# Attention of a two-layer trunk on one core: the products behind the maxima taken for two neighbouring heads at once, each in 64 rows of the contraction

## The chip, the core and the metric

The kernel runs on one core of a Trainium2 chip. Its time is the device time of the whole program in microseconds (us), median of three runs. The engines are named as the profile names them: PE is the matrix engine (PEld its weight loads), DVE the vector engine, ACT the scalar engine, POOL GpSimd, SP the sync engine. All numbers of the program are 32-bit floats. Where an operand has the type `F32R`, PE multiplies in one pass and in reduced precision, and the kernel makes up for that by splitting a value into a high and a low part. Where it has the type `F32`, one product is two passes, which the trace shows as two matmuls.

## What is computed

The reference is a trunk of two layers over 1024 latent tokens (and 256 context tokens) of width 1024. Layer 0 is an mLSTM and convolution mixer, layer 1 is attention, and each has an MLP behind it. The change lies in the attention, which is this:

```
def gqa_attend(q, k, v):
    bsz, nq, _, _ = q.shape
    qg = q.reshape(bsz, nq, KV_HEADS, ATT_HEADS // KV_HEADS, HEAD_DIM)
    s = jnp.einsum('bqhgd,bkhd->bhgqk', qg, k).astype(jnp.float32) * HEAD_DIM ** -0.5
    p = jax.nn.softmax(s, axis=-1).astype(v.dtype)
    o = jnp.einsum('bhgqk,bkhd->bqhgd', p, v)
    return o.reshape(bsz, nq, ATT_HEADS * HEAD_DIM)
```

There are 16 query heads of 64 numbers, 4 key heads (four query heads share one) and 1280 keys: the 1024 latent tokens and the 256 of the context.

## The kernel before

The queries are projected first, in the part of the program that is called the projection below (the loops `for g in range(4)` and `for keep in (2, 1, 0)`, lines 1509 to 1536). `queries` writes each head to `q_d` in device memory as 128 rows: 64 rows of high parts and 64 rows of low parts. The keys lie in `kst[c][:, kv, 0, :]`, where the same 64 high parts stand twice, in rows 0 to 63 and in rows 64 to 127. So one matmul over 128 rows gives (high + low of q) times (high of k).

The attention itself, called the stage below, goes over 32 blocks. A block is one head and one half of the queries: 512 queries against all 1280 keys. Softmax needs the maximum of each query's scores before the exponentials, and the kernel gets it from products of its own, the **score matmuls** of `score` (line 1392): for each group of 128 queries (four of them) and each piece of the keys (`TBS`: 512, 512 and 256 keys) one matmul into a PSUM tile `s`, and one DVE reduction `nm<-s` of that tile to the negated maximum. That is 12 score matmuls and 12 reductions per block: 8 of 512 keys and 4 of 256. `top_of` joins the three pieces, and `rows_of` turns the result into four rows of the operand `qb` (a small F32 matmul `s<-ident,top` into another `s` tile, and a DVE multiply `qb<-s,ident`). The products that the exponentials are taken from, `st`, then carry the subtraction of the maximum inside them.

A block is worked off in five steps (`n` counts all steps, `p` those of a block); a step handles two of the ten key tiles:

- `scores` issues some score matmuls of the next block, as far as the table `BY` allows. It is called at the step's start, once before the first half of `attend`, and once before the second half.
- `part` subtracts the high part of the exponentials of the step before from them, on DVE, where that step is one of `ON_DVE` (p = 1, 3); for the others `probs` gave the subtraction to POOL (`pt<-pf,pt`).
- `probs` issues four `st` matmuls, the exponential `pf<-st` and its rounded copy `pt<-pf` on ACT.
- `attend` issues six `av` matmuls, three per half, for the step three steps back (`LAG`). The second of each three has only 64 columns of weights (`vst[:, at_, 2, :]`).
- At a block's end, ACT takes `av` out of PSUM; after every second block `keep` finishes two heads (`of<-of` on DVE, among others).

So PE has four `st` and six `av` matmuls in every step, 50 in a block, each with 512 columns. They are called **wide matmuls** below.

`InOrder` (`pe_`, `dve_`, `act_`, `pool_`) keeps the instructions of the stage in the order in which the code issues them. The projection and the loads of queries (`load_q`, on POOL's queue) are placed by a scheduler. PSUM has eight banks of 512 numbers per row. In the stage two hold `s` tiles (pool `s`, two buffers of one bank), four hold `st`, two hold `av`. A tile's buffer is given out again when the last reader of its former content is done.

Of the kernel before, what the change touches and what calls it, by code (L numbers as in the profile page):

```python
# [46 lines left out]
def trunk(ctx, tc, a, out):  # L47
    nc = tc.nc
    sp, act, dve, pool, pe = nc.sync, nc.scalar, nc.vector, nc.gpsimd, nc.tensor

    def opened(name, bufs=1, space=None, side=None):
        kw = {"space": space} if space is not None else {}
        if side is not None:
            kw["side"] = side
        return tc.tile_pool(name=name, bufs=bufs, reuse_waits="tile", **kw)
# [4 lines left out]
    hl_pool = ctx.enter_context(opened("hl", 8))  # L60
# [33 lines left out]
    pe_, dve_, act_, pool_ = (InOrder(e) for e in (pe, dve, act, pool))  # L94
# [423 lines left out]
    for half in (1, 0):  # L518
        n = 264
# [307 lines left out]
    for n in range(-3, nv + 3 + BACK):  # L827
# [13 lines left out]
        if done:  # L841
            r = done.pop(0)
# [544 lines left out]
    ap_ = at.enter_context(opened("att", 1, side="right"))  # L1387
    kst = [ap_.tile([P, 4, 2, TBS[b][1]], F32R, name=f"kst{b}") for b in range(3)]
    vst = ap_.tile([P, NTT * 4, 3, 64], F32R, name="vst")
    q_d = dram.tile([16, P, SEQ], F32, name="q_d")  # L1390

    def score(k, qa_, nm, ps, pe, dve):

        i, qt, c = k // 12, k // 3 % 4, k % 3
        kv, n = i % 16 // 4, TBS[c][1]
        pe.matmul(ps[:, 0:n], qa_[:, qt * P:(qt + 1) * P], kst[c][:, kv, 0, :], start=True, stop=True)
        dve.tensor_reduce(out=nm[:, qt, c:c + 1], in_=ps[:, 0:n], axis=AX.X, op=ALU.max, negate=True)

    with opened("rope", 1, side="right") as rp:
        tab = hc_pool.tile([P, 2, 2, 8, 64], F32, name="tab", tag="hc")  # L1400
# [108 lines left out]
        for g in range(4):  # L1509
            wc = load_cols(w_in, 256 * g, 256, dve)  # L1510
            for tt in range(8):
                pq = psum()
                proj_tok(pq, wc, h, tt, 256)
                q2 = heads(pq, tt, 0)
                later(lambda q2=q2, g=g, tt=tt: queries(q2, g, tt), 3)
                if g * 8 + tt < NTT:
                    fill(g * 8 + tt)
                if (g, tt) == (3, 0):
                    ahead = raw_pool.tile([P, 2, 512], F32R, name="ahead", tag="raw")
                    nm0 = ap_.tile([P, 4, 3], F32, name="nm0")  # L1520
                    pool.dma_start(out=ahead, in_=q_d[0:2, :, 0:512].rearrange("h p t -> p h t"))
                if g == 3:
                    for k in range((12 - TAIL) * tt // 8, (12 - TAIL) * (tt + 1) // 8):
                        score(k, ahead[:, 0], nm0, psum(), pe, dve)
                    if tt == 8 - AFTER:
                        wv = load_cols(w_in, 1280, 256)
        k = 12 - TAIL
        for keep in (2, 1, 0):
            if AFTER > 2 - keep:
                pv = psum()  # L1530
                proj_tok(pv, wv, h, 7 - (2 - keep), 256)
                values(7 - (2 - keep), pv)
            later(keep=keep)
            for k in range(k, k + TAIL // 3):
                score(k, ahead[:, 0], nm0, psum(), pe, dve)
            k += TAIL // 3 > 0


# [2 lines left out]
    ps_ctx.close()  # L1541
    wctx.close()
    o_t = [[act_pool.tile([P, KT, 512], F32R, name=f"o{b}{s}", tag="act") for s in "hl"] for b in range(2)]
    with opened("s", 2, PSUM) as scp, opened("st", 2, PSUM) as stp, opened("av", 2, PSUM) as avp, \
            opened("prob", 4, side="right") as bp, opened("sm", 4, side="right") as sm:
        blocks = [(b, hd) for b in range(2) for hd in range(16)]
        nb = len(blocks)
        qa, qb, nms, avs, pts = {}, {}, {}, {}, {}

        def load_q(i):  # L1550
            b, hd = blocks[i]
            qa[i] = bp.tile([P, 512], F32R, name="qa", tag="qa", bufs=3)
            pool.dma_start(out=qa[i], in_=q_d[hd, :, b * 512:(b + 1) * 512])
            nms[i] = sm.tile([P, 4, 3], F32, name="nm", tag="nm")

        def copy_q(i):
            b, hd = blocks[i]
            qb[i] = bp.tile([68, 512], F32R, name="qb", tag="qb", bufs=3)
            act_.copy(out=qb[i][0:64], in_=qa[i][0:64])

        def top_of(i):
            nm = nms[i]
            nms[i] = sm.tile([P, 4], F32, name="top", tag="top")
            dve_.tensor_reduce(out=nms[i], in_=nm, axis=AX.X, op=ALU.min)

        def rows_of(i):

            tp = scp.tile([P, 512], F32, name="s", tag="s")
            pe_.matmul(tp[64:68, 0:P], nms.pop(i), ident, start=True, stop=True)
            dve_.tensor_tensor(out=qb[i][64:68].rearrange("p (j t) -> p j t", j=4), in0=tp[64:68, 0:P].unsqueeze(1).broadcast_to([4, 4, P]),  # L1570
                               in1=ident[64:68, 64:68].unsqueeze(2).broadcast_to([4, 4, P]), op=ALU.mult)

# [51 lines left out]

        NP, LAG, WAIT, ON_DVE = NTT // 2, 3, 1, (1, 3)

        BY = (5, 7, 10, 12, 14)
        outs, ofs, early = [], {}, []
        qa[0], qa[1], nms[0] = ahead[:, 0], ahead[:, 1], nm0
        nms[1] = sm.tile([P, 4, 3], F32, name="nm", tag="nm")  # L1630
        copy_q(0)
        top_of(0)
        rows_of(0)
        pairs = [(i, p) for i in range(nb) for p in range(NP)]
        k = 12

        def scores(upto, n):
            nonlocal k
            for _ in range(n):
                if k < min(upto, 12 * nb):  # L1640
                    score(k, qa[k // 12], nms[k // 12], scp.tile([P, 512], F32, name="s", tag="s"), pe_, dve_)
                    k += 1

        for n in range(len(pairs) + LAG):
            i, p = divmod(n, NP)
            upto = 12 * (i + 1) + BY[p]
            if p == 1 and i + 2 < nb:
                load_q(i + 2)
            if p == 2 and i + 1 < nb:
                copy_q(i + 1)  # L1650
            if (i, p) == (nb - 2, 0):
                early.extend(load_raw(kt_view(a["att_w_out"][0], m * P, P), [KT, P]) for m in range(2))
            if p == 4 and i + 1 < nb:
                top_of(i + 1)
            scores(upto, 1)
            if n and n <= len(pairs):
                part(*pairs[n - 1])
            if n < len(pairs):
                probs(i, p)
# [131 lines left out]
```

## Time and profile before

| what | value |
|---|---|
| time, median of 3 runs | 2942.59 us (2941.59 to 2946.01) |
| the profiled execution's own time | 2953.12 us |
| its span, first to last instruction | 2951.4 us |
| the stage, from 1714 to 2198 us of the span | 484 us |
| PE busy over the span | 96% |
| mean granted clock of PE | 0.974 of full speed |

The page lists each engine's busy time, and further views split it by stretch, by line and by tile. PE's matmuls overlap, so the duration of one (some 0.39 us for a wide one) is longer than the distance from its start to the next one's start. That distance is what a matmul costs PE, and it is read from the timeline. All instructions of the stage stand under line 92, the helper that `InOrder` is made of, so they are told apart by their tiles.

### The profile page before, as it was taken

The page shows a single profiled execution, that of the slowest core. Times are in us where ns is not written, and L with a number is a line of the kernel's source. Part 1 is how long each engine was busy: PE and PEld are TensorE (multiplying, and loading weights), DVE is VectorE, ACT ScalarE, POOL GpSimd, SP SyncE. Part 2 cuts the span into 40 slices and gives each one's busy share as a digit, 9 for nine tenths or more (in the row PEclk, how much of TensorE's full clock was granted, in tenths as well). Part 3 has the DMA queues.
Part 4 walks back from the last instruction along what each step waited for, and adds up shares of the span by engine and source line. Part 5 has one row for each costly group of instructions (what it writes and reads, how often), then busy time and mean ns, then how long its engine had stood idle before and what let it go on. Part 6 is the DMA issues. An engine that isn't in the chain of part 4 may idle for free. (4 is left out here: it accounts for less than half of the span.)

```text
span 2951.4 us, 39291 instructions
## 1 busy us (share of the span) xinstructions
PE 2827.4 (96%) x14523; PEld 2328.2 (79%) x14523; DVE 2030.5 (69%) x3376; ACT 1492.9 (51%) x2556; POOL 691.2 (23%) x564
## 2 busy tenths in 40 slices
PE   7999999988999999999999999999999899989999
PEld 4788998777788888888888977777778688878887
DVE  5445672779876668778787777777756865568886
ACT  5311223455444444444556568888875555544443
POOL 2222424511000000000035545655554000000000
PEclk8999999898999999999999999999999899999999
DMA  6121651344666676332241310000025354474423
GB/s 236 56 73 45 202 153 51 108 146 127 195 190 188 181 243 241 110 136 93 79 144 50 100 52 19 18 19 19 19 80 160 93 175 147 133 288 157 157 93 107
DMA packets 194834, 360.19 MB, mean 122 GB/s; under 512 B 15206, under 2 KB 83666, under 8 KB 194642
## 3 DMA queue, kind: packets, MB, share of 16 engines
q1 hardware_dynamic: 179970, 312.59, 31.4%
q0 software_dynamic: 14672, 45.10, 6.0%
q8 instruction: 114, 1.87, 0.3%
q14 instruction: 78, 0.64, 0.1%
HBM read 260.53 MB, written 97.10 MB: 121 GB/s over the span
## 5 line engine op out<-in xcount | busy, mean ns | idle before, releaser
L338 PE MATMUL ps<-w 128*128 128x512 f32 (+1 forms) x1152 | 424.9, 369 | 0.8 <-DVE w L102 0.8
L339 PE MATMUL ps<-w 128*128 128x512 f32 (+1 forms) x1152 | 424.4, 369 | 0.0
L337 PE MATMUL ps<-w 128*128 128x512 f32 (+1 forms) x1152 | 389.8, 370 | 9.3 <-ACT w L101 9.3
L337 PE MATMUL ps<-tb,w 128*128 128x512 f32 x883 | 351.9, 399 | 15.2 <-ACT u L957 6.2
L339 PE MATMUL ps<-tb,w 128*128 128x512 f32 x888 | 349.6, 397 | 4.0 <-DVE w L102 4.0
L338 PE MATMUL ps<-tb,w 128*128 128x512 f32 x888 | 352.6, 397 | 0.0
L348 DVE SCALAR_TENSOR_TENSOR xT<-ps,mod,xT 128x512 f32<-128x512 f32 (+1 forms) x392 | 255.3, 693 | 87.9 <-PE ps L339 87.5
L92 DVE TENSOR_REDUCE nm<-s 128x1 f32<-128x512 f32 x372 | 217.4, 599 | 106.7 <-PE s L92 101.2
L101 ACT CAST w<-ssum 128x512 fp32r<-128x512 f32 x256 | 155.4, 619 | 258.5 <-PE ps L339 230.7
L92 POOL TENSOR_TENSOR pt<-pf,pt 128x1024 fp32r<-128x1024 f32 x96 | 230.4, 2400 | 171.4 <-ACT pt L92 168.2
L92 PE MATMUL av<-pt,vst 128*128 128x512 f32 (+1 forms) x960 | 257.7, 394 | 0.8 <-POOL pt L92 0.8
L337 PEld LDWEIGHTS ps<-w 128*128 128x128 f32 x1152 | 217.3, 189 | 48.8 <-ACT w L101 10.7
L338 PEld LDWEIGHTS ps<-w 128*128 128x128 f32 x1152 | 218.0, 189 | 40.1 <-DVE w L102 1.2
L339 PEld LDWEIGHTS ps<-w 128*128 128x128 f32 x1152 | 217.3, 189 | 37.7
L906 POOL DMA_DIRECT2D raw<-in_mlp_w_dram x70 | 62.3, 890 | 646.0 <-DVE w L102 301.5
L337 PEld LDWEIGHTS ps<-tb,w 128*128 128x128 f32 x883 | 168.4, 191 | 52.7 <-ACT u L957 7.5
L339 PEld LDWEIGHTS ps<-tb,w 128*128 128x128 f32 x888 | 169.0, 190 | 44.4 <-DVE w L102 5.8
L92 PEld LDWEIGHTS av<-pt,vst 128*128 128x128 f32 (+1 forms) x960 | 159.4, 171 | 56.3 <-POOL pt L92 1.2
L92 ACT ACTIVATE pf<-st 128x1024 f32<-128x1024 f32 x160 | 164.2, 1026 | 75.5 <-PE st L92 68.5
L213 DVE SCALAR_TENSOR_TENSOR aacc<-araw,cw,aacc 128x512 f32<-128x512 f32 x196 | 149.4, 794 | 73.9 <-DMA araw<-in_ada_w_dram 73.3
L338 PEld LDWEIGHTS ps<-tb,w 128*128 128x128 f32 x888 | 169.6, 191 | 35.0
L102 DVE TENSOR_TENSOR w<-ssum,w 128x512 fp32r<-128x512 f32 x256 | 172.5, 682 | 16.3 <-ACT w L101 14.6
(388 smaller groups left out, 6651.8 us busy)
## 6 DMA issues: line engine op xcount, KB each, us to landing
hid<-c SPq DMA_DIRECT2D x224, 256.0 KB
tf<-hid SPq DMA_DIRECT2D x112, 512.0 KB
araw<-in_ada_w_dram SPq DMA_DIRECT2D x72, 512.0 KB
raw<-in_mlp_w_dram POOLq DMA_DIRECT2D x70, 512.0 KB, 5.0
park<-xT SPq DMA_DIRECT2D x32, 512.0 KB
xT<-park SPq DMA_DIRECT2D x32, 512.0 KB
w2e<-in_mlp_w_dram SPq DMA_DIRECT2D x32, 512.0 KB
w2o<-in_mlp_w_dram SPq DMA_DIRECT2D x32, 512.0 KB
```

The costliest lines, as they stand in the source:

```text
L92: return lambda *args, **kw: tc.keep_in_program_order(op(*args, **kw))
L101: (hi_eng or act.copy)(out=hi, in_=src)
L102: (lo_eng or pool).tensor_tensor(out=lo, in0=src, in1=hi.bitcast(F32), op=ALU.subtract)
L213: dve.scalar_tensor_tensor(out=accs[w], in0=r[:, k, :], scalar=c, in1=accs[w], op0=ALU.mult, op1=ALU.add)
L337: pe1.matmul(ps, whi, hhi, start=start, stop=False, skip_group_check=goes_on)
L338: pe.matmul(ps, whi, hlo, start=False, stop=False, skip_group_check=goes_on)
L339: pe.matmul(ps, wlo, hhi, start=False, stop=stop, skip_group_check=goes_on)
L348: dve.scalar_tensor_tensor(out=xT[b][:, m, :], in0=ps[:, 0:n], scalar=mod[layer][:, gate * 8 + m, w:w + 1], in1=xT[b][:, m, :], op0=ALU.mu ...
L906: pool.dma_start(out=r, in_=kt_view(w1, (2 * p + e) * P, P))
```

## The change

`score` now takes the maxima of two neighbouring heads. A tile `qm` of 128 rows holds the high parts of head 2j in rows 0 to 63 and those of head 2j + 1 in rows 64 to 127 (`load_qm`: two loads of 64 rows from `q_d`). Two matmuls, one on each half of the rows, take the place of two on all 128 rows; the low parts of q no longer go into the maximum. The two write the two banks of one `s` tile, and in the stage one DVE reduction reads both and gives both maxima. In the projection there are two `psum` tiles and two reductions.

What goes with it:

- Pool `s` has one buffer of two banks instead of two buffers of one. `rows_of` takes the same buffer.
- The scores run one pair of heads ahead: those of blocks 0 and 1 in the projection (12 pairs of matmuls, where 12 single ones were), and those of blocks 2j + 2 and 2j + 3 while blocks 2j and 2j + 1 are worked off. `BY` has ten entries, one per step of two blocks (`r`). The calls of `scores` are two per step: at its start, and between the halves of `attend`.
- `top_of` runs once for two blocks. `qa` and `qb` have two buffers instead of three, `load_q` is called for the next block instead of the one after it, and `qm` has two buffers. The projection's `qm0` takes a buffer of the pool `hl`.

```
-    def score(k, qa_, nm, ps, pe, dve):
-
-        i, qt, c = k // 12, k // 3 % 4, k % 3
+    def score(k, qm, nm, ps, pe, dve):
+
+
+        i, qt, c = k // 12 * 2, k // 3 % 4, k % 3
         kv, n = i % 16 // 4, TBS[c][1]
-        pe.matmul(ps[:, 0:n], qa_[:, qt * P:(qt + 1) * P], kst[c][:, kv, 0, :], start=True, stop=True)
-        dve.tensor_reduce(out=nm[:, qt, c:c + 1], in_=ps[:, 0:n], axis=AX.X, op=ALU.max, negate=True)
+        for e in range(2):
+            es = slice(e * 64, e * 64 + 64)
+            pe.matmul(ps[e][:, 0:n], qm[es, qt * P:(qt + 1) * P], kst[c][es, kv, 0, :], start=True, stop=True)
+        for e, p in enumerate(ps) if isinstance(ps, list) else ():
+            dve.tensor_reduce(out=nm[:, e, qt, c:c + 1], in_=p[:, 0:n], axis=AX.X, op=ALU.max, negate=True)
+        if not isinstance(ps, list):
+            dve.tensor_reduce(out=nm[:, :, qt, c], in_=ps[2][:, :, 0:n], axis=AX.X, op=ALU.max, negate=True)
+
+    def load_qm(j, qm):
+
+        b, hd = j // 8, j % 8 * 2
+        for e in range(2):
+            pool.dma_start(out=qm[e * 64:(e + 1) * 64], in_=q_d[hd + e, 0:64, b * 512:(b + 1) * 512])
...
-    with opened("s", 2, PSUM) as scp, opened("st", 2, PSUM) as stp, opened("av", 2, PSUM) as avp, \
+    with opened("s", 1, PSUM) as scp, opened("st", 2, PSUM) as stp, opened("av", 2, PSUM) as avp, \
...
-        BY = (5, 7, 10, 12, 14)
+        BY = (1, 3, 4, 5, 7, 8, 9, 11, 12, 12)
...
-                if k < min(upto, 12 * nb):
-                    score(k, qa[k // 12], nms[k // 12], scp.tile([P, 512], F32, name="s", tag="s"), pe_, dve_)
+                if k < min(upto, 6 * nb):
+                    s = scp.tile([P, 2, 512], F32, name="s", tag="s")
+                    score(k, qms[k // 12], nms[k // 12], (s[:, 0], s[:, 1], s), pe_, dve_)
                     k += 1
...
-            upto = 12 * (i + 1) + BY[p]
-            if p == 1 and i + 2 < nb:
-                load_q(i + 2)
+            j, r = divmod(n, 2 * NP)
+            upto = 12 * (j + 1) + BY[r]
+            if p == 1 and 2 <= i + 1 < nb:
+                load_q(i + 1)
+            if r == 6 and 2 * j + 4 < nb:
+                load_pair(j + 2)
...
-            scores(upto, 1)
             if n >= LAG:
                 attend(*pairs[n - LAG], 0)
-            scores(upto, 9)
+            scores(upto)
```

Within two blocks the twelve pairs are numbered 0 to 11 below; pairs 2, 5, 8 and 11 have 256 keys, the others 512. The new table puts this many wide matmuls of PE between one pair and the next: 10 from pair 0 to 1, 7 to pair 2, 3 to pair 3, 10 to pair 4, 10 to pair 5; then 4, the first `top` matmul, and 3 to pair 6; 3 to pair 7, 10 to pair 8, 10 to pair 9, 7 to pair 10, 3 to pair 11; then 14, the second `top` matmul, and 6 to the next pair 0.

PE at the end of a block's last `st` matmuls, before: one `top` matmul, then single score matmuls, and up to six wide ones between them.

```order
L92 MATMUL s<-ident,top 4x128 [waits DVE_49]
L92 MATMUL s<-kst_13927,qa 128x512 [waits DVE_49]
L92 MATMUL av<-pt,vst 128x512
L92 MATMUL av<-pt,vst 64x512
L92 MATMUL av<-pt,vst 128x512 x2
L92 MATMUL av<-pt,vst 64x512
L92 MATMUL av<-pt,vst 128x512
L92 MATMUL s<-kst_13928,qa 128x256 [waits DVE_49]
L92 MATMUL st<-qa,kst_13926 128x512 [waits Activation_49]
```

The same place now, at the middle of two blocks: the `top` matmul and pairs 6 and 7, each of which waits for DVE with its first matmul.

```order
L92 MATMUL s<-ident,top 4x128 [waits DVE_49]
L92 MATMUL av<-pt,vst 128x512
L92 MATMUL av<-pt,vst 64x512
L92 MATMUL av<-pt,vst 128x512
L92 MATMUL s<-kst_13926,qm 128x512 [waits DVE_49]
L92 MATMUL s<-kst_13926,qm 128x512
L92 MATMUL av<-pt,vst 128x512
L92 MATMUL av<-pt,vst 64x512
L92 MATMUL av<-pt,vst 128x512
L92 MATMUL s<-kst_13927,qm 128x512 [waits DVE_49]
L92 MATMUL s<-kst_13927,qm 128x512
```

What moved: the score matmuls now come in pairs with three wide matmuls between them here, and all of them, with the `top` matmul, pass through one buffer.

DVE over the same stretch, before: `pt` is `part`'s subtraction and `qb` the multiply of `rows_of`.

```order
L92 TENSOR_TENSOR pt<-pf,pt 128x1024 [waits Activation_49,Pool_49]
L92 TENSOR_TENSOR qb<-s,ident 4x512 [waits PE_49]
L92 TENSOR_REDUCE nm<-s 128x1 [waits PE_49] x7
L92 TENSOR_TENSOR pt<-pf,pt 128x1024 [waits Activation_49,Pool_49]
L92 TENSOR_REDUCE nm<-s 128x1 [waits PE_49] x4
```

And now, from pair 4's reduction to pair 11's:

```order
L92 TENSOR_REDUCE nm<-s 128x2 [waits PE_49]
L92 TENSOR_TENSOR of<-of 128x512 [waits Activation_49]
L92 TENSOR_REDUCE nm<-s 128x2 [waits PE_49]
L92 TENSOR_TENSOR pt<-pf,pt 128x1024 [waits Activation_49,Pool_49]
L92 TENSOR_TENSOR qb<-s,ident 4x512 [waits PE_49]
L92 TENSOR_REDUCE nm<-s 128x2 [waits PE_49] x4
L92 TENSOR_TENSOR pt<-pf,pt 128x1024 [waits Activation_49,Pool_49]
L92 TENSOR_REDUCE nm<-s 128x2 [waits PE_49] x2
```

What moved: half as many reductions, each of two maxima. `pt`, `qb` and `of` still stand between them, and the buffer that they hold up is the only one.

## Rows read from the trace of the kernel before

**Rows 1.** Busy time of each engine in a stretch: the projection's end, and 100 us of the stage.

```profile
core 0: us, PE busy (x) PEld busy (x) DVE busy (x) ACT busy (x) POOL busy (x), PEclk, DMA share, GB/s
1640.00:1714.00 74.00, 69.08 (x568) 68.28 (x566) 55.34 (x98) 35.79 (x102) 38.51 (x62) 0.98 0.32 92
1760.00:1860.00 100.00, 98.63 (x429) 72.26 (x429) 71.73 (x111) 83.49 (x94) 58.85 (x30) 1.00 0.07 19
```

**Rows 2.** Timeline of PE: the `top` matmul of two blocks, 22 blocks apart.

```profile
1774.23 0.38 PE L92 MATMUL s<-ident,top 128*4 128x128 f32 x2
...
2103.00 0.38 PE L92 MATMUL s<-ident,top 128*4 128x128 f32 x2
```

**Rows 3.** Timeline of PE, and matmuls by form: wide matmuls and a score matmul of 256 keys.

```profile
1801.37 0.28 PE L92 MATMUL s<-kst,qa 128*128 128x256 f32 x1
1801.49 1.55 PE L92 MATMUL av<-pt,vst 128*128 128x512 f32 x6
1802.88 0.40 PE L92 MATMUL s<-kst,qa 128*128 128x512 f32 x1
...
L92 PE MATMUL av<-pt,vst 128*64 128x512 f32 x320 | 126.2, 394 | 0.0
```

**Rows 4.** Timeline of PE around one `top` matmul.

```profile
1803.82 0.40 PE L92 MATMUL st<-qb,kst 68*128 68x512 f32 x1
1804.15 0.38 PE L92 MATMUL s<-ident,top 128*4 128x128 f32 x2
1804.46 0.50 PE L92 MATMUL s<-kst,qa 128*128 128x512 f32 x1
1804.79 0.40 PE L92 MATMUL av<-pt,vst 128*128 128x512 f32 x1
```

**Rows 5.** Timeline of PE early in the program: full matmuls, then 32-column ones.

```profile
109.82 0.40 PE L339 MATMUL ps<-h0h,wlo 128*128 128x512 f32 x1
110.15 0.62 PE L170 MATMUL ps<-raw,cw 128*32 128x512 f32 x2
...
147.62 0.28 PE L339 MATMUL ps<-h2h,wlo 128*128 128x256 f32 x1
147.83 0.62 PE L170 MATMUL ps<-raw,cw 128*32 128x512 f32 x2
```

**Rows 6.** Timeline of PE in layer 0: F32 matmuls on 64 rows and on 128.

```profile
520.87 0.27 PE L775 MATMUL ps<-cn,aq 64*128 64x129 f32 x1
521.07 0.49 PE L773 MATMUL ps<-va,ub 128*128 128x129 f32 x2
521.49 0.37 PE L775 MATMUL ps<-cn,aq 64*128 64x129 f32 x1
521.50 0.37 PE L733 MATMUL ps<-qT,kT 64*128 64x128 f32 x1
```

**Rows 7.** DVE's groups in the stage, 1714 to 2198 us.

```profile
L92 DVE TENSOR_REDUCE nm<-s 128x1 f32<-128x512 f32 x248 | 170.7, 689 | 97.1 <-PE s L92 95.4
L92 DVE TENSOR_TENSOR pt<-pf,pt 128x1024 fp32r<-128x1024 f32 x64 | 78.4, 1225 | 14.3 <-ACT pt L92 11.5 <-issue 0.3
L92 DVE TENSOR_TENSOR of<-of 128x512 f32<-128x512 f32 x15 | 16.9, 1124 | 21.1 <-ACT of L92 21.1
```

**Rows 8.** Timeline of DVE beside rows 3 and 4.

```profile
1801.69 0.42 DVE L92 TENSOR_REDUCE nm<-s 128x1 f32<-128x256 f32 x1 [0.37 <-PE s L92]
...
1803.32 0.69 DVE L92 TENSOR_REDUCE nm<-s 128x1 f32<-128x512 f32 x1 [1.00 <-PE s L92]
...
1805.41 0.69 DVE L92 TENSOR_TENSOR qb<-s,ident 4x512 fp32r<-4x512 f32 x1
```

**Rows 9.** Timeline of PE's weight loads: the first that waits for that `qb`.

```profile
1806.15 0.19 PEld L92 LDWEIGHTS s<-kst,qa 128*128 128x128 f32 x1 [0.23 <-DVE qb L92]
```

**Rows 10.** POOL's loads of queries: time on POOL, KB and us to landing.

```profile
L1553 POOL DMA_DIRECT2D qa<-q_d x27 | 15.3, 569 | 26.5 <-PE st L92 25.0 <-PE s L92 1.5
...
qa<-q_d POOLq DMA_DIRECT2D x30, 256.0 KB, 3.0
```

**Rows 11.** Timeline of PE where the stage begins.

```profile
1714.09 0.38 PE L92 MATMUL s<-ident,top 128*4 128x128 f32 x2 [2.40 <-DVE top L92]
```

More of the change, by code (lines that the diff above doesn't have):

```diff
@@ L1519, in trunk @@
                     ahead = raw_pool.tile([P, 2, 512], F32R, name="ahead", tag="raw")
-                    nm0 = ap_.tile([P, 4, 3], F32, name="nm0")
+                    nm0 = ap_.tile([P, 2, 4, 3], F32, name="nm0")
+                    qm0 = hl_pool.tile([P, 512], F32R, name="qm0", tag="hl")
+                    load_qm(0, qm0)
                     pool.dma_start(out=ahead, in_=q_d[0:2, :, 0:512].rearrange("h p t -> p h t"))
@@ L1523, in trunk @@
                     for k in range((12 - TAIL) * tt // 8, (12 - TAIL) * (tt + 1) // 8):
-                        score(k, ahead[:, 0], nm0, psum(), pe, dve)
+                        score(k, qm0, nm0, [psum(), psum()], pe, dve)
                     if tt == 8 - AFTER:
@@ L1534, in trunk @@
             for k in range(k, k + TAIL // 3):
-                score(k, ahead[:, 0], nm0, psum(), pe, dve)
+                score(k, qm0, nm0, [psum(), psum()], pe, dve)
             k += TAIL // 3 > 0
@@ L1547, in trunk, with load_pair, top_of @@
         nb = len(blocks)
-        qa, qb, nms, avs, pts = {}, {}, {}, {}, {}
+        qa, qb, qms, nms, tops, avs, pts = {}, {}, {}, {}, {}, {}, {}
         def load_q(i):
             b, hd = blocks[i]
-            qa[i] = bp.tile([P, 512], F32R, name="qa", tag="qa", bufs=3)
+            qa[i] = bp.tile([P, 512], F32R, name="qa", tag="qa", bufs=2)
             pool.dma_start(out=qa[i], in_=q_d[hd, :, b * 512:(b + 1) * 512])
-            nms[i] = sm.tile([P, 4, 3], F32, name="nm", tag="nm")
+        def load_pair(j):
+            qms[j] = bp.tile([P, 512], F32R, name="qm", tag="qm", bufs=2)
+            load_qm(j, qms[j])
+            nms[j] = sm.tile([P, 2, 4, 3], F32, name="nm", tag="nm")
         def copy_q(i):
             b, hd = blocks[i]
-            qb[i] = bp.tile([68, 512], F32R, name="qb", tag="qb", bufs=3)
+            qb[i] = bp.tile([68, 512], F32R, name="qb", tag="qb", bufs=2)
             act_.copy(out=qb[i][0:64], in_=qa[i][0:64])
[L1561 to L1564, printed above, removed]
+        def top_of(j):
+            top = sm.tile([P, 2, 4], F32, name="top", tag="top")
+            dve_.tensor_reduce(out=top, in_=nms.pop(j), axis=AX.X, op=ALU.min)
+            tops[2 * j], tops[2 * j + 1] = top[:, 0], top[:, 1]
         def rows_of(i):
             tp = scp.tile([P, 512], F32, name="s", tag="s")
-            pe_.matmul(tp[64:68, 0:P], nms.pop(i), ident, start=True, stop=True)
+            pe_.matmul(tp[64:68, 0:P], tops.pop(i), ident, start=True, stop=True)
             dve_.tensor_tensor(out=qb[i][64:68].rearrange("p (j t) -> p j t", j=4), in0=tp[64:68, 0:P].unsqueeze(1).broadcast_to([4, 4, P]),
@@ L1625, in trunk @@
         NP, LAG, WAIT, ON_DVE = NTT // 2, 3, 1, (1, 3)
-        BY = (5, 7, 10, 12, 14)
+        BY = (1, 3, 4, 5, 7, 8, 9, 11, 12, 12)
         outs, ofs, early = [], {}, []
         qa[0], qa[1], nms[0] = ahead[:, 0], ahead[:, 1], nm0
-        nms[1] = sm.tile([P, 4, 3], F32, name="nm", tag="nm")
+        load_pair(1)
         copy_q(0)
@@ L1635, in trunk, with scores @@
         k = 12
-        def scores(upto, n):
+        def scores(upto, n=9):
             nonlocal k
             for _ in range(n):
-                if k < min(upto, 12 * nb):
-                    score(k, qa[k // 12], nms[k // 12], scp.tile([P, 512], F32, name="s", tag="s"), pe_, dve_)
+                if k < min(upto, 6 * nb):
+                    s = scp.tile([P, 2, 512], F32, name="s", tag="s")
+                    score(k, qms[k // 12], nms[k // 12], (s[:, 0], s[:, 1], s), pe_, dve_)
                     k += 1
@@ L1652, in trunk @@
                 early.extend(load_raw(kt_view(a["att_w_out"][0], m * P, P), [KT, P]) for m in range(2))
-            if p == 4 and i + 1 < nb:
-                top_of(i + 1)
+            if r == 9 and i + 1 < nb:
+                top_of(j + 1)
             scores(upto, 1)
```

## The prediction

> **What bounds the kernel now.** Read the busy time of the stretches first [rows 1]. In the stage PE is busy 98.6 of 100 us at full clock, ACT 83, DVE 72, POOL 59. So PE sets the pace, and a change in the stage is worth what it does to PE's time, its own work and its waits. Next, the pace: the `top` matmuls of blocks 22 apart start 328.77 us apart [rows 2], 14.94 us per block, 29.89 us per two. Then the timeline of PE, for what one matmul costs. From the first of six `av` matmuls to the score matmul behind them are 1.39 us, 0.232 each, called a step of PE; a score matmul of 256 keys takes 0.12 [rows 3]. Around a `top` matmul [rows 4] the starts lie 0.33, 0.31 and 0.33 apart. The first 0.33 is the distance to an instruction of another shape (4 columns instead of 128). The second holds both passes of `top`. The third is 0.10 more than a step: the score matmul's weights, which could not be loaded ahead. So one `top` costs 0.97 - 2 x 0.232 = 0.5 us.
>
> Two blocks before, then: 100 wide matmuls 23.2, 16 score matmuls of 512 keys 3.7, 8 of 256 keys 1.0, two `top` 1.0, in all 28.9 us. The measured 29.9 leaves 1.0 us of waits.
>
> **The change, part by part.**
>
> *A pair of matmuls on 64 rows.* Three things have a price. First, do the two run side by side? In layer 0 the last matmul of L775 works on rows 64 to 127 and the first of L733 on rows 0 to 63; they start 0.01 us apart [rows 6]. I take it that a pair costs one step. Second, what does it cost to go from full matmuls to 64-row ones and back? From full matmuls to 32-column ones the distance is 0.33 after 512 columns and 0.21 after 256, with no wait [rows 5], against steps of 0.232 and 0.12: 0.10 until the array is empty. 0.10 more goes to weights that then load in the open, as behind `top` [rows 4]. With 64 rows it is the same in both directions: L775 to L773 0.20, and from L773's second pass (521.07 + 0.49 - 0.27 = 521.29) to L775 0.20 again, after 129 columns, about as much as after 256 in rows 5 [rows 6]. Third, is that so for F32R? The `av` matmuls of 64 columns are F32R, between full ones, and cost a plain step [rows 3]. That speaks for no price at all. I follow the 64-row rows, since the `av` matmuls differ in columns and the new ones in rows, and keep both ends: 0 and 0.40 us per pair.
>
> The Trainium skill, TensorEngine Tiling (Array Packing), Key Properties, says that changing the tiling mode drains the TensorE, which speaks against this change; rows 5 and 6 agree, the `av` matmuls of rows 3 don't. The Trainium skill, PSUM — Partial Sum Buffer, The four PSUM rules, says that float32r matmuls force the full column group. That would explain `av` and leaves the rows open: by it the price stays as I took it.
>
> With the price a pair of 512 keys takes 0.33 (from the last wide matmul) + 0.43 (weights 0.10, stream and drain 0.33) + 0.33 (the next wide matmul), less the two steps that the wide ones cost anyway: 0.62 us, where two single matmuls took 0.46. A pair of 256 keys takes 0.12 less (rows 5: 0.33 against 0.21), 0.50, where two took 0.24. Per two blocks: 8 x 0.16 + 4 x 0.26 = **+2.3 us**.
>
> *One `s` buffer instead of two.* A pair may start only when the reduction of the pair before is done. A reduction takes 0.69 for 512 numbers [rows 7] and 0.42 for 256 [rows 8]. One of 1024 is not in the trace; continued in a line it is 1.24, and the subtraction of 1024 numbers takes 1.225 [rows 7]. I take 1.23; the ends are 0.69 (the second bank free) and 1.38 (two of 512). From a matmul's end to its reduction are 0.04 us (1802.88 + 0.40 to 1803.32), from DVE's end to the weight load that waited 0.05 (1806.10 to 1806.15) [rows 3, 8, 9]. So a pair holds the buffer for 0.10 + 0.40 + 0.04 + 1.23 + 0.05 = 1.82 us, of 256 keys 0.10 + 0.28 + 0.04 + 0.69 + 0.05 = 1.16. With m wide matmuls between, PE itself comes to the next pair 0.43 + 0.10 + (m - 1) x 0.232 + 0.33 after the last: 1.32 for m = 3, 2.25 for 7, 2.95 for 10; 0.12 less after a pair of 256. Now the places, from the list ahead of the fences:
> - m = 10 and 7: no wait for the buffer. Pair 2 to 3: 1.20 against 1.16, none.
> - Pair 6 to 7: 1.82 - 1.32 = 0.5.
> - Pair 10 to 11: 0.5 again. Besides, `pt` (1.225) stands on DVE between the reductions of 9 and 10, so that the latter starts 0.2 late: 0.7.
> - Pair 5, `top`, pair 6: the buffer passes through the reduction of 5, which ends after 1.11, then `pt` and `qb` on DVE, 1.225 and 0.69, so it is free after some 3.1. PE comes after 0.31 + 0.10 + 0.70 + 0.33 (to `top`) + 0.31 + 0.90 = 2.65. That is 0.45. The reduction of 5 stands behind `of`, which waits 21.1/15 = 1.4 us for ACT now [rows 7], and `pt` waits for its rounded copy. I take 0.9 for the place.
>
> In all 2.1 us of waits where 1.0 was, **+1.1 us**. PE works in order, so the `st` and `av` matmuls behind stand too, and ACT's exponentials with them; ACT has 16 us in 100 to spare [rows 1].
>
> *DVE.* Per two blocks 8 x 1.23 + 4 x 0.69 = 12.6 us of reductions where 16 x 0.69 + 8 x 0.42 = 14.4 stood. DVE isn't the bound, so its 1.8 us are worth nothing but the waits above.
>
> *Loads.* Two more issues on POOL per two blocks, 0.57 us each [rows 10], beside POOL's 41% of idle time [rows 1]. The loads wait for their buffer at the head of POOL's queue, with subtractions behind them, as now (25.0 us in 26 waits [rows 10]). A head's queries land after 3.0 us [rows 10]; ACT copies them about a block (15 us) after the issue, so fewer buffers cost nothing. If that cover were gone, ACT would stand up to 3 us in each block.
>
> *The sum in the stage.* +2.3 + 1.1 = +3.4 us per two blocks. The last two blocks have no scores left to take: 15 x 3.4 = 51, less one block's 12 single matmuls and waits (8 x 0.232 + 4 x 0.12 + 0.5 = 2.8): **+48 us**.
>
> *The projection.* 12 pairs stand where 12 single matmuls stood: 8 x (0.62 - 0.23) + 4 x (0.50 - 0.12) = 4.6 us, one pair is torn apart by the scheduler and pays twice (0.4), and DVE has 12 more reductions, 8 x 0.69 + 4 x 0.42 = 7.2 us, in a stretch where it idles 19 of 74 us [rows 1]. Where the stage begins PE already waits 2.40 us for DVE's `top` [rows 11]; I put 1 to 3 us of the 7.2 there. **+7 us.**
>
> Together +55 us. From the profiled execution's 2953.12 us that is 3008; that execution lies 10.5 us (0.36%) above the median shown, so on the median's scale 2942.59 + 55, some **2998 us**.
>
> **The rivals.**
> - *Two full matmuls in all but name*: F32R on 64 rows behaves as the 64-column `av` does, neither side by side nor with a change of shape. For it: rows 3. PE's work stays, and the buffer alone costs: held 1.96 us (two steps, then the reduction), PE at the next pair after 1.16 for m = 3, so 0.8 at pair 7, some 1.2 at 11, 0.25 at 3 and 1.2 at 6: 3.4 where 1.0 was. 15 x 2.4 - 3, with 12 more matmuls (2.3) and some DVE in the projection: +38, 2981 us.
> - *Change of shape, but one after the other*: 8 x 0.232 + 4 x 0.12 = 2.3 us more per two blocks than my sum: +90, 3033 us. Against it: rows 6.
> - *Side by side without a change of shape*: PE's work falls by 2.3 us per two blocks. The Trainium skill, TensorEngine Tiling (Array Packing), Theoretical Speedup, gives up to 2x for a contraction of 64, which is this rival; no F32R row here shows it. It decides at the buffer: the kernel is faster as long as the waits stay under 2.3 + 1.0 = 3.3 us per two blocks. The walk above, with 0.93 us between pairs for m = 3, gives 0.8 + 0.25 + 1.4 + 1.2 = 3.7, and so about 2947 us. If DVE, 1.8 us lighter, kept the waits at 1.0, it would be 2942.59 - 15 x 2.3 - 3 = 2905 us, faster.
>
> **How the numbers follow.** My forecast has 0.66; two full matmuls 0.12; one after the other 0.07; side by side without a change of shape 0.15, of which 0.05 is faster, 0.04 about the same and 0.06 slower. A measurement of this kernel can tell about 0.2% (6 us). So faster 0.05, same 0.04, slower 0.91. The forecast's own bounds: a reduction of 1.38 adds 0.15 at three places, +7 us; one of 0.69 takes nearly all waits away, -30. The range takes these, two full matmuls, and reaches towards the one after the other: 2966 to 3034, with some 0.2 left out.
>
> **What would show it.** In the changed kernel's stage: two blocks take some 33.3 us, the stage about 532. The matmuls `s<-kst,qm` on 64 rows come in twos, 0.01 us apart (steps of 0.23 would mean one after the other); the wide matmul behind a pair starts 0.43 after it, and the weight load of a pair 0.33 after the last wide one where nothing is waited for. Reductions of 128x1024 take 1.23. PE's weight loads wait for DVE's `nm` and `qb` some 30 us in all, longest before pairs 6, 7 and 11. I am wrong if a pair follows a wide matmul after 0.23, if the waits lie elsewhere (ACT for `st`, POOL), or if the projection grows by over 10 us.

## The result, and the profile after

| | before | changed |
|---|---|---|
| time, median | 2942.68 us (2941.59 to 2946.01) | 3015.39 us (3011.46 to 3023.09) |
| the profiled execution's own time | 2953.12 us | 3023.09 us |
| first `st` matmul to the first matmul of the output projection | 482.4 us | 556.6 us |
| two blocks of the stage, at granted clock 1.00 throughout | 29.9 us | 34.1 us |

The changed kernel takes 1.0248 times as long (95%: 1.0226 to 1.0270), 72.7 us more. The forecast was slower by 55, with a range of 2966 to 3034 us: sign and range hold, the size falls 17 us short.

Where did the time go? The profiled executions are 70.0 us apart. From the first `st` matmul to the output projection they differ by 74.3 us. From the last matmul on the context's keys (1541.90 us before, 1536.29 after) to the first `st` matmul (1714.74 and 1712.28) it is 172.84 and 175.99 us, 3.2 more. The rest, which the change doesn't touch, happens to be 7.5 us shorter in this execution. So it is the stage, and there first the pace, the time from a `top` matmul to the second one after it. Timeline of PE, changed kernel, the `top` matmuls of two blocks that are two apart (start, duration, engine, line, operation, tiles, shapes):

```profile
1925.26 0.38 PE L92 MATMUL s<-ident,top 128*4 128x128 f32 x2
...
1959.35 0.38 PE L92 MATMUL s<-ident,top 128*4 128x128 f32 x2
```

34.09 us, where [rows 2] give 29.89: 4.2 more for each of 15 such pairs of blocks, 63 us. The last blocks, which have no scores left, give 2.6 back. That leaves 14 us of the 74, and they are in the clock. Busy time by stretch, changed kernel: four blocks, each from its `top` matmul to the next (odd ones begin with the `top` in the middle of two), then two pieces of the first of them:

```profile
core 0: us, PE busy (x) PEld busy (x) DVE busy (x) ACT busy (x) POOL busy (x), PEclk, DMA share, GB/s
1797.78:1818.74 20.96, 18.83 (x64) 11.32 (x64) 9.52 (x10) 12.70 (x15) 10.53 (x7) 0.84 0.07 18
1907.20:1925.26 18.06, 15.91 (x64) 9.56 (x64) 9.51 (x10) 12.70 (x15) 10.59 (x7) 1.00 0.07 20
1925.26:1941.28 16.02, 15.86 (x66) 9.56 (x65) 10.46 (x10) 12.37 (x14) 7.74 (x5) 1.00 0.10 27
1941.28:1959.35 18.07, 15.94 (x64) 9.56 (x65) 9.52 (x10) 12.70 (x15) 10.57 (x7) 1.00 0.09 21
...
1797.78:1801.90 4.12, 2.68 (x10) 1.14 (x10) 3.07 (x3) 2.81 (x4) 3.54 (x3) 1.00 0.23 64
1801.90:1808.70 6.80, 6.67 (x16) 4.28 (x17) 1.99 (x3) 2.07 (x2) 2.82 (x2) 0.50 0.00 0
```

Even and odd blocks take 16.02 and 18.07 us; the extra 2 us are PE's waits (PE is busy 15.9 us in both). One odd block takes 20.96: in it the granted clock is 0.50 for 6.8 us, 1.2 instead of 2.4 GHz. In the 4.1 us before that, which hold most of the waits described next, PE is busy for 2.7. Six odd blocks of the profiled execution are stretched like this, to 19.6 to 21.0 us, together 14 us over 18.05; the stretch at 0.50 begins 2.9 to 4.8 us after the `top`, at or just behind the waits of pairs 6 and 7. For the kernel before [rows 1] show 1.00, and so does the rest of its stage from the third block on.

Now the waits. Timeline of PE, changed kernel, from pair 5 over a `top` to pair 7:

```profile
1939.67 0.39 PE L92 MATMUL s<-kst,qm 64*128 64x256 f32 x2
1939.99 0.50 PE L92 MATMUL st<-qa,kst 128*128 128x512 f32 x1
1940.32 0.40 PE L92 MATMUL st<-qb,kst 68*128 68x512 f32 x1
...
1940.79 0.40 PE L92 MATMUL st<-qb,kst 68*128 68x512 f32 x1
1941.28 0.38 PE L92 MATMUL s<-ident,top 128*4 128x128 f32 x2
1941.59 0.97 PE L92 MATMUL av<-pt,vst 128*128 128x512 f32 x3
1943.70 0.50 PE L92 MATMUL s<-kst,qm 64*128 64x512 f32 x2 [1.14 <-DVE qb L92]
1944.13 0.96 PE L92 MATMUL av<-pt,vst 128*128 128x512 f32 x3
1945.53 0.50 PE L92 MATMUL s<-kst,qm 64*128 64x512 f32 x2 [0.43 <-DVE nm L92]
```

The two matmuls of a pair stand in one row, "x2", with the duration of one (0.50): they run side by side. The wide matmul behind pair 6 starts 0.43 later, as forecast. `top` starts 0.49 after the last `st`, 0.16 more than in [rows 4]. Pair 6 should follow the third `av` (1942.16) by 0.33 and follows by 1.54: 1.20 us of waiting. Pair 7 starts 1.83 us after pair 6, the forecast's 1.82 for which a pair holds the buffer, and 0.50 later than it could. What DVE does meanwhile, same kernel:

```profile
1939.50 1.12 DVE L92 TENSOR_TENSOR of<-of 128x512 f32<-128x512 f32 x1 [1.02 <-ACT of L92]
1940.55 0.68 DVE L92 TENSOR_REDUCE nm<-s 128x2 f32<-128x512 f32 x1
1941.70 1.22 DVE L92 TENSOR_TENSOR pt<-pf,pt 128x1024 fp32r<-128x1024 f32 x1 [0.47 <-ACT pt L92]
1942.95 0.69 DVE L92 TENSOR_TENSOR qb<-s,ident 4x512 fp32r<-4x512 f32 x1
1944.24 1.23 DVE L92 TENSOR_REDUCE nm<-s 128x2 f32<-128x1024 f32 x1 [0.60 <-PE s L92]
```

All of this stands in one queue: `of` waits 1.02 for ACT, so the reduction of pair 5 is late and with it `top`; `pt` waits 0.47 for ACT's rounded copy, and `qb`, which frees the buffer, stands behind it until 1943.64. Besides, pair 11 waits 0.62 and the pair behind the other `top` 0.15. Together 2.6 us in two blocks. Over the whole stage, in the waits of the changed kernel (engine, what waits, releaser: us in total, times, longest):

```profile
PEld s L92 <- DVE nm L92: 43.6, 63, 1.1
...
PEld s L92 <- DVE qb L92: 31.3, 30, 1.6
```

The groups in the stage, changed kernel: a reduction of 1024 takes 1.225 us, one of 2 x 256 0.689, as forecast (for one of 512 see [rows 7]).

```profile
L92 DVE TENSOR_REDUCE nm<-s 128x2 f32<-128x1024 f32 x118 | 144.5, 1225 | 103.3 <-PE s L92 103.3
...
L92 DVE TENSOR_REDUCE nm<-s 128x2 f32<-128x512 f32 x59 | 40.7, 689 | 60.2 <-PE s L92 60.2
```

### The profile page after: what moved, and what is told of

It reads as the page before. It is cut to its first block, busy times and chain, and to the rows that moved or that the text cites. A ratio compares the mean times of both kernels' runs of the same rounds, so it can differ in the third digit from the quotient of the medians.

```text
span 3021.3 us, 39177 instructions
## 1 busy us (share of the span) xinstructions
PE 2872.3 (95%) x14523; PEld 2297.8 (76%) x14523; DVE 2006.9 (66%) x3180; ACT 1492.6 (49%) x2556; POOL 705.6 (23%) x596
## 5 line engine op out<-in xcount | busy, mean ns | idle before, releaser
L92 DVE TENSOR_REDUCE nm<-s 128x2 f32<-128x1024 f32 x180 | 188.4, 1046 | 167.1 <-PE s L92 167.1
L92 PE MATMUL av<-pt,vst 128*128 128x512 f32 (+1 forms) x960 | 272.4, 413 | 0.7 <-POOL pt L92 0.7
```

Source lines behind the costliest of these rows:

```text
L92: return lambda *args, **kw: tc.keep_in_program_order(op(*args, **kw))
```

## The experiments

The theory: per two blocks the change of shape costs PE 2.3 us, the one buffer some 1.9 us of waits, and the waits bring the clock down now and then. The rivals: (1) the buffer is all of it; (2) the shape is all of it; (3) the 64-row matmuls themselves bring the clock down. Pairs are counted 0 to 11 in two blocks. Wherever two blocks are compared they are undisturbed ones, at granted clock 1.00. The kernel before ran again beside each set: 2947.0 us for runs 1 to 4, 2945.0 for 5 to 8, 2945.4 for 9. The ratios are to that, with the 95% interval.

**1. The pairs at other places.** `BY` says how many pairs are taken by the end of each of ten steps.

```
-        BY = (1, 3, 4, 5, 7, 8, 9, 11, 12, 12)
+        BY = (1, 3, 4, 5, 6, 7, 9, 10, 12, 12)
```

> The pairs stay on 64 rows with one buffer and one maximum; only their places move: the two places with three wide matmuls to the next pair now lie behind pairs of 256 keys, none lies behind a `top`. Theory (change of shape and buffer waits add up): the work keeps its +2.4 us per two blocks, the waits fall from 2.6 us to the 0.1 to 0.5 behind `top`: two blocks 31.6 to 32.0 us where they took 34.07, and the time is 2942.6 + 15 x 1.9 - 3 + 3 for the projection = 2971 us (2963 to 2980). Rival 1 (the buffer is all of it): two blocks 29.5, some 2945 us. Rival 2 (the pairs themselves, the buffer hardly counts): 3005 to 3015 us. On the clock: if it falls because PE waits, the granted clock is 1.00 in every stretch of the stage from its second block on; if 64-row matmuls bring it down, the spells at half speed stay.

Measured: 2983.3 us, 1.0122 (1.0105 to 1.0138), 32.07 us per two blocks. `top` matmuls, then the stage by stretches of 100 us (columns as above):

```profile
1904.92 0.38 PE L92 MATMUL s<-ident,top 128*4 128x128 f32 x2
...
1936.99 0.38 PE L92 MATMUL s<-ident,top 128*4 128x128 f32 x2
```

```profile
1740.00:1840.00 100.00, 98.40 (x401) 59.83 (x400) 62.28 (x63) 78.91 (x89) 57.57 (x35) 1.00 0.10 27
1840.00:1940.00 100.00, 98.10 (x400) 59.32 (x399) 62.66 (x63) 77.54 (x87) 56.72 (x36) 1.00 0.11 30
```

Only 0.16 us ahead of one `top` and 0.51 behind it are left of the waits. So 2 of the 4.2 us per two blocks were waits that another order avoids, and without them the clock stays at 1.00 with the same 64-row pairs, from the second block to the last but one. (In the last block, behind a wait of 1.63 us for `qb`, 3.4 us run at 0.50.) Rival 1 falls, since 36 us over the kernel before remain, and so does rival 2, since the order alone took away about as much. The time lies 3 us above the range given, of which the kernel before, 4 us slower beside this set, accounts for all; the pace lies 0.1 above.

**2. Both matmuls on all rows.**

```
-            es = slice(e * 64, e * 64 + 64)
-            pe.matmul(ps[e][:, 0:n], qm[es, qt * P:(qt + 1) * P], kst[c][es, kv, 0, :], start=True, stop=True)
+            es = slice(0, P)
+            pe.matmul(ps[e][:, 0:n], qm[es, e, qt * P:(qt + 1) * P], kst[c][es, kv, 0, :], start=True, stop=True)
```

`qm` holds both heads whole, [P, 2, 512], loaded at once and kept in the pool `raw`, since the pool of `qm` has no room.

> Both matmuls of a pair run on all 128 rows, as the single ones did, with the changed kernel's order, one buffer and one maximum. Theory: no change of shape, so 2.4 us of work per two blocks go; but the two run one after the other, the buffer is held 0.13 longer and PE, with no drain, is at the next pair 0.16 earlier for three wide matmuls between, 1.16 us where it is held 1.96: waits of 0.8, 0.9 and 0.25 at these places and some 1.9 around `top`, 3.9 in all. Two blocks 32.6 to 33.6 us, the time 2942.6 + 15 x 3.2 - 3 + 1 = 2989 us (2979 to 3000). Rival 1 (the shape change is all): two blocks 29.9 to 30.5, 2943 to 2952 us. Rival 2 (the buffer is all): 3015 us as the changed kernel. On the clock: spells at half speed if waits bring it down, none if the 64-row matmuls do.

Measured: 3005.9 us, 1.0200 (1.0185 to 1.0216).

```profile
1996.38 0.38 PE L92 MATMUL s<-ident,top 128*4 128x128 f32 x2 [0.52 <-DVE nm L92]
...
1998.80 0.74 PE L92 MATMUL s<-kst,qm 128*128 128x512 f32 x2 [1.14 <-DVE qb L92]
...
2000.86 0.73 PE L92 MATMUL s<-kst,qm 128*128 128x512 f32 x2 [0.63 <-DVE nm L92]
...
2030.11 0.38 PE L92 MATMUL s<-ident,top 128*4 128x128 f32 x2 [0.51 <-DVE nm L92]
```

33.73 us per two blocks. PE has as much work as before the change and loses its gain to the buffer: the two matmuls run one after the other, hold it longer, and PE is back sooner. The clock falls here too, with no 64-row matmul in the stage:

```profile
1740.00:1840.00 100.00, 90.89 (x373) 63.67 (x372) 59.19 (x60) 72.51 (x82) 52.21 (x29) 0.97 0.11 29
1840.00:1940.00 100.00, 92.00 (x371) 64.32 (x370) 56.20 (x57) 71.90 (x80) 52.16 (x30) 0.95 0.12 32
```

So 64-row matmuls aren't needed to bring it down (rival 3). The time lies 6 us above the range, 4 of them as in run 1; the pace is 0.1 above: the waits were again sized too small.

**3. Other places and all rows**, the edits of 1 and 2 together.

> 128 rows and the moved places together, still one buffer and one maximum. Theory: work 28.9 us per two blocks, and the waits that one buffer leaves even so: 0.25 at the two places behind pairs of 256 keys, 0.1 where six wide matmuls stand between, 0.3 to 0.5 at each `top`: two blocks 30.0 to 31.3 us, 2942.6 + 15 x 0.8 - 3 + 1 = 2953 us (2943 to 2965). So the shape change alone, moved places in both, is worth 10 to 36 us (against the first run). Rival (the shape change costs nothing by itself): the same as the first run within 5 us.

Measured: 2975.3 us, 1.0097 (1.0082 to 1.0112).

```profile
1930.69 0.38 PE L92 MATMUL s<-ident,top 128*4 128x128 f32 x2
...
1962.21 0.38 PE L92 MATMUL s<-ident,top 128*4 128x128 f32 x2
```

31.52 us, a miss: 30.0 to 31.3 was expected, and the time lies 10 us above its range. Of the 31.52, 2.4 us are waits: 0.58 ahead of one `top`, 0.63 behind it, 0.43 behind the other, 0.25 at each of the two pairs that follow one of 256 keys, and the rest where the second matmul of such a late pair starts 0.34 behind the first, not 0.23. Against run 1 taking the shape away gains 8 us, not 10 to 36, since waits for the buffer take its place; so a difference of two such runs doesn't price the shape.

**4. Two maxima instead of one.**

```
-            dve.tensor_reduce(out=nm[:, :, qt, c], in_=ps[2][:, :, 0:n], axis=AX.X, op=ALU.max, negate=True)
+            [dve.tensor_reduce(out=nm[:, e, qt, c:c + 1], in_=ps[2][:, e, 0:n], axis=AX.X, op=ALU.max, negate=True) for e in range(2)]
```

> The changed kernel with two reductions per pair instead of one; the buffer is still freed as a whole. Theory: a reduction of 2 x 512 takes 2 x 0.69 = 1.38 where one of 1024 took 1.23, so each wait for the buffer grows by 0.15: four places, 0.6 us per two blocks, and the undisturbed two blocks take 34.5 to 34.7; 3015.4 + 15 x 0.5 = 3023 us (3016 to 3030). Rival (one maximum is the cost, two short ones free the first bank sooner): 3000 us or less.

Measured: 3025.1 us, 1.0262 (1.0246 to 1.0278). Two reductions behind each other, in DVE's timeline:

```profile
1963.71 1.29 DVE L92 TENSOR_REDUCE nm<-s 128x1 f32<-128x512 f32 x2 [0.62 <-PE s L92]
```

1.29 us, not 1.38: they overlap a little. Two undisturbed blocks take 34.23 us, less than the 34.5 to 34.7 expected: 0.14 more than in the changed kernel, 2 us in all. Over the kernel before it is 78 us, 5 more than the change; the other 3 us the pace doesn't explain, and they lie within the spread of the runs (3018 to 3028). The one maximum is no cost, and worth little.

**5. Both matmuls on rows 0 to 63.** As in run 2, with

```
+            es = slice(0, 64)
```

> Both matmuls of a pair on rows 0 to 63, the changed kernel's order, one buffer, one maximum: the shape changes as before, but the two share their rows. Theory: they run one after the other, the second 0.23 us behind the first (0.12 for 256 keys), so 8 x 0.23 + 4 x 0.12 = 2.3 us more per two blocks; up to 0.5 of it is taken back where PE waits for `qb` behind `top`, which was late anyway. Two blocks 35.8 to 36.4 us, 3015 + 15 x (1.7 to 2.3) = 3041 to 3050 us. Rival (the starts 0.003 us apart are only how records look, and the pair streams one after the other already): 3015 us, two blocks 34.1.

Measured: 3045.4 us, 1.0343 (1.0325 to 1.0360), 35.79 us per two blocks.

```profile
1980.90 0.73 PE L92 MATMUL s<-kst,qm 64*128 64x512 f32 x2
1981.57 0.50 PE L92 MATMUL st<-qa,kst 128*128 128x512 f32 x1
```

On the same rows two matmuls last 0.73 us where the pair of the change lasts 0.50, and the next wide one starts 0.67 behind the first, not 0.43. So the pairs of the change do run side by side.

**6. Single matmuls on 64 rows, two buffers**, in the kernel before:

```
-        pe.matmul(ps[:, 0:n], qa_[:, qt * P:(qt + 1) * P], kst[c][:, kv, 0, :], start=True, stop=True)
+        pe.matmul(ps[:, 0:n], qa_[0:64, qt * P:(qt + 1) * P], kst[c][0:64, kv, 0, :], start=True, stop=True)
```

> The kernel of before, two buffers, single score matmuls, but each on the 64 rows of the high part alone (the low part of the queries is left out of the maxima). Theory: one matmul on 64 rows between full ones costs as much as a pair, 0.62 us for 512 keys and 0.50 for 256, where it cost 0.232 and 0.12: 24 x 0.39 = 9.3 us more per two blocks, less up to 1.0 of waits; two blocks 38.2 to 39.2 us, 2945 + 15 x (8.3 to 9.3) + 12 x 0.39 in the projection = 3074 to 3089 us. Rival 1 (the price comes from two at once, or from one buffer): 2945 to 2965 us. Rival 2 (one matmul pays half of a pair's price): 2965 to 3000 us. On the clock: no spell at half speed if it is waits that bring it down.

Measured: 3070.1 us, 1.0432 (1.0418 to 1.0447), 37.91 us per two blocks, no wait of PE and no stretch at half speed in the steady stage.

```profile
1942.33 0.40 PE L92 MATMUL st<-qb,kst 68*128 68x512 f32 x1
1942.66 0.49 PE L92 MATMUL s<-kst,qa 64*128 64x512 f32 x1
1943.09 1.18 PE L92 MATMUL av<-pt,vst 128*128 128x512 f32 x4
```

0.33 ahead, 0.43 behind: one 64-row matmul costs what two side by side cost. Against run 8, the kernel before free of waits, it is 8.76/24 = 0.365 us each where 0.39 was expected, so pace and time lie just below their ranges (by 0.3 and 4 us). Two of them stand beside `top` and may share its change of shape; that this is the difference is not shown.

**7. Run 1, and `pt` behind `qb`.**

```
-            if n and n <= len(pairs):
+            if n and n <= len(pairs) and p != 4:
                 part(*pairs[n - 1])
...
             if p == 4 and i + 1 < nb:
                 rows_of(i + 1)
+            if n and n <= len(pairs) and p == 4:
+                part(*pairs[n - 1])
```

> The first run's places, and DVE's subtraction for `pt` stands behind the one for `qb` at each `top`, so that the pair behind `top` finds its buffer free. Theory: the 0.5 us of wait that the first run left behind one `top` of two goes, 0.2 may stay ahead of it; the price of the shape change stays whole: two blocks 31.4 to 31.7 us, 2983 - 15 x (0.35 to 0.65) = 2973 to 2978 us. Rival (what is left over the kernel before is still waiting): 2960 us or less.

Measured: 2978.6 us, 1.0115 (1.0101 to 1.0128).

```profile
1903.85 0.38 PE L92 MATMUL s<-ident,top 128*4 128x128 f32 x2
...
1935.39 0.38 PE L92 MATMUL s<-ident,top 128*4 128x128 f32 x2
```

31.54 us, with one wait of 0.15 left. This is the price of the shape by itself: 31.4 us of work.

**8. The kernel before, with `pt` behind `qb` as in run 7, and other places:**

```
-        BY = (5, 7, 10, 12, 14)
+        BY = (5, 8, 11, 12, 13)
```

> The kernel of before with the same subtraction behind `qb` and its score matmuls at other places (5, 8, 11, 12, 13 by the five steps instead of 5, 7, 10, 12, 14). Theory: of the 1.0 us of waits per two blocks, all of them at `top`, 0.3 to 0.7 go: two blocks 29.2 to 29.6 us, 2945 - 15 x (0.3 to 0.7) = 2934 to 2940 us. Rival (PE's waits there are for something else): no difference.

Measured: 2938.6 us against 2945.0, 0.9979 (0.9967 to 0.9990): the fastest of all, ahead of both kernels, by a little.

```profile
1917.83 0.38 PE L92 MATMUL s<-ident,top 128*4 128x128 f32 x2
...
1946.98 0.38 PE L92 MATMUL s<-ident,top 128*4 128x128 f32 x2
```

29.15 us with no wait: this is the work of the kernel before, against which the work in runs 2 to 7 is read. The pace gains 0.74 us per two blocks, 11 us over the stage; 6.4 arrive, and what takes the rest is open.

**9. `pt` behind `qb` alone**, in the changed kernel.

> The changed kernel with its own places; alone DVE's subtraction for `pt` stands behind the one for `qb` at each `top`. Theory: `qb` starts 1.27 us earlier, so the pair behind `top` starts without its wait of 1.20 us; but its reduction then stands behind the subtraction for `pt` (until some 3.6 us after `top` began to be late), so the wait of 0.50 before the next pair grows to about 1.1. Of 1.7 us at this place 0.4 to 0.7 are gained: two blocks 33.4 to 33.7 us, 3015 - 15 x (0.4 to 0.7) = 3005 to 3009 us. Rival (the wait behind `top` is worth all of its 1.20): 32.9 us, 2997 us or less. On the clock: a wait of about 1 us remains in every second block, so spells at half speed stay; if only the place behind `top` brings them, they go.

Measured: 3014.9 us, 1.0234 (1.0217 to 1.0251), nothing gained; 34.13 us per two blocks. PE, then DVE, in this kernel:

```profile
1939.09 0.50 PE L92 MATMUL s<-kst,qm 64*128 64x512 f32 x2
...
1942.48 0.49 PE L92 MATMUL s<-kst,qm 64*128 64x512 f32 x2 [2.01 <-DVE nm L92]
```

```profile
1938.31 0.69 DVE L92 TENSOR_TENSOR qb<-s,ident 4x512 fp32r<-4x512 f32 x1 [0.47 <-PE s L92]
1939.03 2.14 DVE L92 TENSOR_TENSOR pt<-pf,pt 128x1024 fp32r<-128x1024 f32 x1
1941.20 1.23 DVE L92 TENSOR_REDUCE nm<-s 128x2 f32<-128x1024 f32 x1
```

33.4 to 33.7 us were expected, a miss. Pair 6 indeed no longer waits, and pair 7 waits 2.0 us instead of 0.43: the wait moved by one pair, and more of it than I had worked out, because the subtraction took 2.14 us for its usual 1.22. A moved wait is worth something only where the next user of the buffer isn't near; in run 7, where no pair stood close behind, the same edit gained its 0.5 us.

## Why the prediction was right, and what it mis-sized

- *The change of shape, +2.3 us per two blocks*: right. 31.4 us of work (run 7) against 29.15 (run 8) is 2.2 to 2.3, some 34 us over the stage. F32R on 64 rows does run side by side (run 5) and does pay for the change of shape (run 6). I had kept a bound of 0 open because the 64-column `av` of [rows 3] pay nothing; for rows they don't speak. The Trainium skill, TensorEngine Tiling (Array Packing), Key Properties, says that a change of mode drains the TensorE. The rows of run 6, 0.33 and 0.43 us where 0.23 is a plain step, agree.
- *One `s` buffer, +1.1 us*: right in kind and place, too small. Pair 7 waits 0.50 (0.5 forecast) and pair 11 0.62 (0.7). The step that failed is "I take 0.9 for the place" of pair 5, `top` and pair 6: it measured 0.16 + 1.20 = 1.36. I had counted that `of` and `pt` wait for ACT, but not for how long: the buffer that pair 5 takes at 1939.67 comes free for pair 6 only 4.0 us later, not 3.1. What sets this is `pt`, which starts when ACT's rounded copy is there (0.47 after the reduction of pair 5), with `qb` behind it in the queue; of the 1.02 that `of` waits only the 0.16 ahead of `top` reach PE. The 0.15 behind the other `top` I had not seen. The waits are 2.6 us, not 2.1, and those of the kernel before 0.74 (29.89 less run 8's 29.15), not 1.0: +1.9 where +1.1 stood, some 11 us over the stage.
- *The clock*: a term that was missing. I took the granted clock of 1.00 [rows 1] for the changed stage as well. Between the stage's first two blocks and its last one, the profiled executions of the kernels whose PE waits little (0 to 0.8 us in two blocks: before, runs 1, 6, 7, 8) show 1.00; each of the others (some 2 to 4.6 us: the change, runs 2, 3, 4, 5, 9) has one to six stretches at 0.50. In the changed kernel's they cost 14 us. That waits go with it and 64 rows don't is shown by runs 1, 2 and 6; what decides in which block it falls is open: run 9 has as much waiting as the changed kernel and two stretches where that has six.
- *The projection, +7 us*: 3.2 in the profiled execution. Most of DVE's further reductions lay under PE's work; PE's idle time hardly grew, and the wait for `top` where the stage begins only from 2.40 [rows 11] to 3.09 us, as PE's timeline of the changed kernel shows:

```profile
1710.19 0.59 PE L92 MATMUL s<-ident,top 128*4 128x128 f32 x2 [3.09 <-DVE top L92]
```

  The pairs themselves cost more than the 3.2 let see, because less of this stretch ran at half clock. Busy time by stretch, columns as above, the kernel before and then the changed one:

```profile
1541.90:1714.74 172.84, 160.58 (x1301) 158.67 (x1300) 127.25 (x220) 99.05 (x267) 90.65 (x134) 0.96 0.28 80
```

```profile
1536.29:1712.28 175.99, 163.38 (x1314) 156.72 (x1313) 134.25 (x232) 99.37 (x267) 93.87 (x139) 0.97 0.30 86
```

  The kernel before ran 13.7 us of it at 0.50, the changed one 9.4. Half of the difference, 2 us, is an estimate of what this hid; with it the projection grew by some 5 us, about what the prediction gave the pairs alone.
- *DVE* worth nothing, *loads* hidden: right. DVE's reduction times are those forecast, and no pair waits for a load.
- *What would show it*: pairs in twos, 0.33 and 0.43 around them, 1.23 for the reduction, the longest waits before pairs 6, 7 and 11, all as said. The stage took 557 us, not 532, two blocks 34.1 for 33.3, and the weight loads wait 75 us for `nm` and `qb`, not 30 (by the same view PE itself stands for 32 of them; in the rest its earlier matmuls still run).
- *The rivals*: two full matmuls in all but name is run 2, and I had priced it at 2981 us where it takes 3006: the same undersized waits (3.4 for 33.73 - 29.15 = 4.6 us). One after the other is run 5: 3045 measured, 3033 given. Side by side without a change of shape isn't what this chip does with these rows.

Of the 17 us that were missing, then, some 11 are waits; the projection took 4 less than its term; the 10 that remain I put down to the clock. That is less than the 14 of the profiled execution, which is the slowest of the four: its mean granted clock over the whole program is 0.969, that of the other three 0.973 to 0.977, and no trace shows where theirs fell. That the range holds the result is in part luck: its upper end was drawn for a slower reduction and for a rival, not for longer waits and a falling clock.

## What to carry to other kernels

Two matmuls on half the rows each take the time of one, but a change of shape costs about 0.4 us of PE around it, so a lone pair of 512 columns between full matmuls costs more (0.62 us) than two full ones in a row (0.46). By these numbers two pairs behind one another would cost some 0.85 us where four full ones cost 0.93, an estimate that no run here tried: pack rows only where several packed pairs can follow one another, and count the PSUM banks that this needs first. Where a buffer is halved in number, walk its chain through the in-order queue of the engine that frees it, and ask for every instruction in it when its own input is ready: the latest sets the wait (here `pt`'s). And when waits appear on a PE that was always busy, look for a further price in granted clock; here spacing the users of the buffer (run 1) took most of both away.

## What was not expected of the hardware

DVE's subtraction for `pt` (three operands in SBUF) takes 1.2 us in all 64 cases of the kernels before and after. In runs 7 and 9, where it stands later, 15 of 64 take 1.9 to 2.2. In run 9 POOL's subtraction for `o0l` has just begun; the changed kernel's, where DVE is first, is the longer one. Timeline of POOL, run 9 and then the changed kernel:

```profile
1938.80 1.29 POOL L92 TENSOR_TENSOR o0l<-of,o0h 128x512 fp32r<-128x512 f32 x1 [0.36 <-ACT o0h L92]
```

```profile
1942.20 1.85 POOL L92 TENSOR_TENSOR o0l<-of,o0h 128x512 fp32r<-128x512 f32 x1 [0.37 <-ACT o0h L92]
```

In run 9 POOL runs from 1938.80 to 1940.09 and DVE's, begun at 1939.03, ends at 1941.17, 0.9 us late; in the changed kernel DVE runs from 1941.70 to 1942.92 and POOL's, begun at 1942.20, takes 0.56 longer. The one that starts second is held up until about the end of the first. In all eleven traces the elementwise instructions of the stage with two inputs in SBUF (`pt` on either engine, `of` on DVE, `o0l` and `o1l` on POOL) keep to this: the later one is longer by what the earlier one has left when it starts, less some 0.14 us (to within 0.05), and it keeps its usual time where less than that is left. Other operations were not tried.

This bears on the wait ahead of `top`. `of` takes 0.69 us in the one case of each kernel in which no such instruction of POOL runs beside it, and 1.11 to 1.13 in the other 15, before and after the change, which all begin while POOL's `pt` has 0.56 to 0.59 us left. So `of` ends 0.43 us late, and the reduction of pair 5 behind it too; by an estimate from these rows that is all of the 0.16 us by which `top` comes late.

The matmul behind the first one of a new shape also comes late: `st` to `st` behind a pair is 0.34 us (1945.96 to 1946.30 in PE's timeline of the changed kernel) where 0.23 is a plain step. Why is not shown. This tenth of a microsecond is part of the pair's 0.62 us.
